# A hybrid attention and recurrence layer: two recurrent groups in step, values for four heads at once, gated outputs through DRAM, halves apart in the last output block

## The chip, the cores and the metric

The kernel runs on one core of a Trainium2 chip. The metric is the device time of one launch in microseconds, lower is better. A core has five engines with their own instruction streams: TensorE (PE in the profile; its weight loads are PEld), VectorE (DVE), ScalarE (ACT), GpSimd (POOL) and SyncE (SP), which here issues nearly all transfers. Each engine works through its stream in order and waits on semaphores for the others.

## The reference

One layer over 256 frames of width 4096, all in float32. An input projection of `x` feeds two groups of heads and a gate:

```
proj = x @ w_in                      # fox q|k|v|f, rwkv r|k|v|w_down|a_down, gate z
fox:   logits[t,s] = q_t.k_s/sqrt(128) + sum_{s<j<=t} log f_j ; softmax over s <= t ; times v      (16 heads of 128)
rwkv:  r,k,v,wd,ad are mixed with the frame before (mu_shift); decay and rate come from low-rank products
       S_t = S_{t-1} diag(w_t) + (S_{t-1} a_t) b_t^T + v_t k_t^T ;  y_t = S_t r_t                  (32 heads of 64)
       a = -kk, b = kk * rate, kk = normalised k*k_k ; GroupNorm per head of y, plus a bonus (r.k.r_k) v
h   = concat(fox, rwkv) * silu(z)
out = LayerNorm(2**0.25 * x + h @ w_out)
```

## The kernel before

**Tiling.** A group is 128 columns: one fox head and two rwkv heads; there are 16 groups. `x` lies transposed in SBUF as 32 tiles `xs[k]` of 128 x 256 frames, each split into a high and a low float32r part (2 x 256 columns). A weight tile of 128 x 1024 is fetched by SP (`fetch`, lines 206 to 211; four raw buffers `wr`), cast to its high part by ACT (line 134) and subtracted to its low part by DVE (line 135); three pairs of these are held. `mm` (lines 138 to 140) makes one k-step of a projection: the high weights times both parts of `x` (512 columns), the low weights times the high part (256 columns). `proj(i, j)` (line 221) runs 32 such k-steps for one group and one of eight projections: r, k, v of the recurrence, q, k, v of fox, and the gates of fox and rwkv.

**Side work.** All else that the mixing needs is written as Python generators (`front`, `rwkv`, `fox`). `slot()` (line 193) is called after every four k-steps and advances each generator to its next `yield`, so that its instructions are written between the projections' matmuls; `wait(n)` lets n slots pass, and the table `W` holds these numbers. The framework then orders each engine's stream by a planner that simulates durations and takes what is ready first in the order written; `keep_in_program_order` pins single instructions.

**The recurrence.** `rwkv(i)` works in four chunks of 64 frames for the two heads of one group, j = 0 and 1 on partitions 0 to 63 and 64 to 127. In order: norms `np` (lines 410, 411), Gram products `gp` (427), centred values `vp` (433), transposes `tp` (436); the masks (444, 453); the strictly lower blocks go to DRAM as `nd` and come back broadcast as `Nb`; a triangular solve by 31 row steps on DVE (473, 476); its result goes to DRAM as `td` and comes back as `T` (480, 483); `qt` (493) and `xp` (512) complete the inverses `X`. Then for each chunk: `rh` (502) is copied to `R` by DVE (504); `up` (525) is copied to `UV`, half by DVE (526) and half by ACT (527); `sp` (532) updates the state `SV` (537, 541); `yp` (544) gathers the outputs. After that the GroupNorm with `vs` (556, 557), and `gate` (330), which keeps every gated output `h` in SBUF. These small products are in plain float32 and show as two matmul records each; those of the two heads use different halves of the array.

**fox** (567) transposes its head's values (`fvp`, 577), makes the logits (`fsp`, 581 and 582), the softmax, its transposes (`fpt`, 595) and the output (`fop`, 600 and 601).

**The output.** Eight blocks of 512 columns (line 666). Each runs 32 k-steps of six matmuls of 512 columns (681 to 683), three for each half m of the frames. In the first block `get_h` (637) splits each `h` into its parts; the tail of the last group's recurrence is still between its matmuls. After the last block: the sums of both halves (696, 697), moments (709), a small row product by which mean and bias go in (721, 729), the scaling on DVE (730) and the stores (732, 735).

Of the kernel before, what the change touches and what calls it, by code (L numbers as in the profile page):

```python
# [17 lines left out]
P = 128  # L18
# [18 lines left out]
ROWS = 2  # L37
W = {"fr": 10, "fo": 3, "vs": 2, "np": 6, "gp": 5, "d1": 10, "d2": 10, "xp": 3, "fs": 4, "fp": 5}
# [39 lines left out]
def layer(ctx: ExitStack, tc: tile.TileContext, xt, xtok, w_lora, w_main, w_o, up, par, mulora, fbias, lng, lnb, cst, out, groups=G, dbg=None):  # L78
# [52 lines left out]
    def split(src, n, name):  # L131
        hi = wpool.tile([P, 1024], F32R, tag="wh", name=name + "h")
        lo = wpool.tile([P, 1024], F32R, tag="wl", name=name + "l")
# [44 lines left out]
    X = const.tile([P, NCH, P], F32, name="X")  # L178
    nc.gpsimd.memset(X, 0.0)
    gb = [const.tile([P, NCH, P], F32, name=f"gb{j}") for j in range(2)]  # L180
    for j in range(2):
        nc.gpsimd.memset(gb[j], 0.0)
# [17 lines left out]
    stream = [(f"w{i}_{j}_{q}", w_main[i, j][:, 8 * q : 8 * q + 8, :]) for i in range(groups) for j in range(8) for q in range(4) if i or j]  # L200
    if dbg is None:
        stream += [(f"wo{b}_{q}", w_o[b][:, 2 * q : 2 * q + 2, :]) for b in range(NB) for q in range(KT // 2)]
    stream.reverse()
    ready = []

    def fetch():
        if stream:
# [3 lines left out]
            ready.append((name, *split(raw, 1024, name)))  # L211
# [20 lines left out]

    mid = ctx.enter_context(ExitStack())
    hpool = mid.enter_context(tc.tile_pool(name="hpool", bufs=1))
    rp = mid.enter_context(tc.tile_pool(name="rp", bufs=1))

# [25 lines left out]

    def shifted(acc, n, i):
        name = f"s{n}_{i}"
        r = t256(f"s{n}", name)
# [53 lines left out]
    szs = {}  # L319

    def silu2(acc, key):
# [4 lines left out]
        sz = t256("sz" + key[0], key + "s")  # L326
# [3 lines left out]
    def gate(y, key, k):  # L330
        h = hpool.tile([P, S], F32, tag=f"h{k}", name=f"h{k}")
        nc.vector.scalar_tensor_tensor(h, y, 0.5, szs[key], ALU.mult, ALU.mult)
        hs[k] = h
# [12 lines left out]

    pre = {}
    done = set()

    def front(i):  # L350
# [22 lines left out]
        eL = rp.tile([P, NCH, C + 1], F32, tag="eL", name=f"eL{i}", bufs=2)  # L373
# [9 lines left out]
        pre[i] = (eL, eI, am, ae)  # L383

    def rwkv(i):
        while i not in pre or (i, 1) not in rk:
            yield
        eL, eI, am, ae = pre[i]
        r, kr = rk[i, 0], rk[i, 1]
        k = rt(f"k{i}")  # L390
# [388 lines left out]
```

## Time and profile before

| | |
|---|---|
| median of 3 runs (lowest, highest) | 2037.81 us (2037.07, 2040.23) |
| the profiled execution: its own time, its span | 2038.04 us, 2036.2 us |
| granted TensorE clock, mean | 0.996 |
| busy: PE, PEld, DVE, ACT, POOL | 2019.8, 1709.0, 1465.5, 1026.4, 27.6 us |
| data moved | 372.71 MB, mean 183 GB/s |

How to read it: the span runs from the first to the last instruction; the program's own time is 1.8 us more. PE counts as busy while a matmul is under way, and the matmuls overlap, so a row's duration (0.39 us for 512 columns) is not what a matmul costs: that is the distance between the starts of two rows. In the timeline a row is: start, duration, engine, line, operation, out<-in, shapes, how many were merged; idle time before it in brackets.

### The profile page before, as it was taken

How to read it: one execution, taken by the hardware profiler on the slowest of the kernel's cores; microseconds unless marked ns; L12 is line 12 of the kernel's file. 1: busy time of each engine (PE TensorE's matmuls, PEld its weight loads, DVE VectorE, ACT ScalarE, POOL GpSimd, SP SyncE). 2: the span in 40 equal slices, each digit the busy share in tenths (PEclk: the TensorE clock that was granted, in tenths of full speed). 3: DMA queues.
4: the chain of work that ended last, by engine and by line, in shares of the span. 5: the costliest groups of instructions: out<-in, count | busy, mean ns of one | idle time of the engine just before them, and what ended most of it. 6: DMA issues, size and time to landing. Idle time of an engine off the chain costs nothing.

```text
span 2036.2 us, 32893 instructions
## 1 busy us (share of the span) xinstructions
PE 2019.8 (99%) x12426; PEld 1709.0 (84%) x12426; DVE 1465.5 (72%) x2921; ACT 1026.4 (50%) x1609; POOL 27.6 (1%) x138
## 2 busy tenths in 40 slices
PE   9999999999999999999999999999999999999997
PEld 7888888888888888888888888888888888888885
DVE  7877777777777777777777777777777796655555
ACT  6645454545454545454545454545454564433332
POOL 0000000000000000000000000000000000000000
PEclk9999999999999999999999999999999999999998
DMA  8555555555555555555555555555555557866664
GB/s 288 181 178 177 173 178 172 179 173 177 172 177 172 179 171 179 172 179 173 178 174 177 174 177 175 175 175 173 176 172 176 172 173 243 261 194 191 186 205 145
DMA packets 131295, 372.71 MB, mean 183 GB/s; under 512 B 31208, under 2 KB 40600, under 8 KB 131136
## 3 DMA queue, kind: packets, MB, share of 16 engines
q1 hardware_dynamic: 130704, 370.19, 57.8%
q8 instruction: 97, 1.59, 0.3%
q10 hardware_dynamic: 432, 0.43, 0.1%
q14 instruction: 62, 0.51, 0.1%
HBM read 364.23 MB, written 6.32 MB: 182 GB/s over the span
## 4 chain that ended last, share of the span: by engine, by line
PE 96%; DVE 2%; DMA 1%; issue 0%; ACT 0%; SPq 0%; DVEq 0%
PE acc L139 47%; PE acc L140 23%; PE oacc L681 6%; PE oacc L682 6%; PE oacc L683 6%; PE yp L544 1%; PE gp L427 1%; PE rh L502 1%; PE sp L532 1%; PE accl L139 1%; PE up L525 1%; DMA xr<-in_xt_dram 1%; DVE res L730 0%; PE vp L433 0%; PE tp L436 0%
## 5 line engine op out<-in xcount | busy, mean ns | idle before, releaser
L139 PE MATMUL acc<-x,w_2h 128*128 128x512 f32 x1016 | 377.0, 408 | 0.0
L139 PE MATMUL acc<-x,w_1h 128*128 128x512 f32 x1016 | 369.7, 402 | 0.0
L139 PE MATMUL acc<-x,w_3h 128*128 128x512 f32 x1016 | 369.6, 401 | 0.0
L139 PE MATMUL acc<-x,w_0h 128*128 128x512 f32 x1016 | 365.5, 399 | 0.0
L140 PE MATMUL acc<-x,w_1l 128*128 128x256 f32 x1016 | 285.8, 281 | 0.0
L140 PE MATMUL acc<-x,w_3l 128*128 128x256 f32 x1016 | 284.8, 280 | 0.0
L140 PE MATMUL acc<-x,w_2l 128*128 128x256 f32 x1016 | 284.7, 280 | 0.0
L140 PE MATMUL acc<-x,w_0l 128*128 128x256 f32 x1016 | 284.6, 280 | 0.0
L139 PEld LDWEIGHTS acc<-x,w_1h 128*128 128x128 f32 x1016 | 190.7, 188 | 45.6
L139 PEld LDWEIGHTS acc<-x,w_3h 128*128 128x128 f32 x1016 | 190.7, 188 | 44.5
L139 PEld LDWEIGHTS acc<-x,w_0h 128*128 128x128 f32 x1016 | 190.7, 188 | 44.2
L139 PEld LDWEIGHTS acc<-x,w_2h 128*128 128x128 f32 x1016 | 190.9, 188 | 43.5
L134 ACT CAST w_0h<-w 128x1024 fp32r<-128x1024 f32 x127 | 133.4, 1050 | 170.1 <-PE acc L139 136.5
L135 DVE TENSOR_TENSOR w_2l<-w,w_2h 128x1024 fp32r<-128x1024 f32 x127 | 155.4, 1223 | 80.5 <-ACT w_2h L134 80.2
L134 ACT CAST w_2h<-w 128x1024 fp32r<-128x1024 f32 x127 | 133.4, 1050 | 153.4 <-PE acc L139 140.5
L140 PEld LDWEIGHTS acc<-x,w_3l 128*128 128x128 f32 x1016 | 191.9, 189 | 0.6
L140 PEld LDWEIGHTS acc<-x,w_2l 128*128 128x128 f32 x1016 | 192.1, 189 | 0.5
L135 DVE TENSOR_TENSOR w_0l<-w,w_0h 128x1024 fp32r<-128x1024 f32 x127 | 155.3, 1223 | 50.9 <-ACT w_0h L134 49.8
L140 PEld LDWEIGHTS acc<-x,w_1l 128*128 128x128 f32 x1016 | 191.9, 189 | 0.0
L140 PEld LDWEIGHTS acc<-x,w_0l 128*128 128x128 f32 x1016 | 191.8, 189 | 0.0
L135 DVE TENSOR_TENSOR w_1l<-w,w_1h 128x1024 fp32r<-128x1024 f32 x127 | 155.2, 1222 | 49.1 <-ACT w_1h L134 49.0
L134 ACT CAST w_1h<-w 128x1024 fp32r<-128x1024 f32 x127 | 132.8, 1046 | 110.8 <-issue 57.6
(703 smaller groups left out, 3240.4 us busy)
## 6 DMA issues: line engine op xcount, KB each, us to landing
w<-in_w_main_dram SPq DMA_DIRECT2D x508, 512.0 KB
wo<-in_w_o_dram SPq DMA_DIRECT2D x128, 512.0 KB
Nb<-nd SPq DMA_DIRECT2D x16, 512.0 KB
res<-in_xtok_dram SPq DMA_DIRECT2D x16, 256.0 KB
out_dram<-res SPq DMA_DIRECT2D x7, 512.0 KB
xr<-in_xt_dram SPq DMA_DIRECT2D x6, 512.0 KB
lr<-in_w_lora_dram SPq DMA_DIRECT2D x6, 416.0 KB
nb<-ncd SPq DMA_DIRECT2D x16, 128.0 KB
```

Of the source, the lines that this page charges most:

```text
L134: nc.scalar.copy(hi[:, :n], src[:, :n])
L135: nc.vector.tensor_tensor(lo[:, :n], src[:, :n], hi[:, :n].bitcast(F32), ALU.subtract)
L139: nc.tensor.matmul(acc[:m, :], hi[:, o : o + m], xs[k].rearrange("p a t -> p (a t)"), start=(k == 0), stop=False)
L140: nc.tensor.matmul(acc[:m, :S], lo[:, o : o + m], xs[k][:, 0, :], start=False, stop=(k == KT - 1))
L427: nc.tensor.matmul(gp[j][:, c * P : (c + 1) * P], BK[h, c, :], lt[j][h, c, :], start=True, stop=True)
L502: nc.tensor.matmul(rh[HALF[j], :C], lt[j][:, c, 0:C], SV[j][:, c, :], start=True, stop=True)
L525: nc.tensor.matmul(upp[:, :C], X[:, c, :], R, start=True, stop=True)
L532: nc.tensor.matmul(sp[HALF[j], :C], BKt[:, c, j * C : (j + 1) * C], UV[j][:, c, :], start=True, stop=True)
L544: nc.tensor.matmul(yp[HALF[j], c * C : (c + 1) * C], lhs[j][:, c, :], rhs[j][:, c, C:P], start=lhs is SV, stop=lhs is UV)
L681: nc.tensor.matmul(acc[m], ht[k][:, 0, tt], hi[:, o], start=(k == 0), stop=False)
L682: nc.tensor.matmul(acc[m], ht[k][:, 1, tt], hi[:, o], start=False, stop=False)
L683: nc.tensor.matmul(acc[m], ht[k][:, 0, tt], lo[:, o], start=False, stop=(k == KT - 1))
```

## The change

Six parts.

1. **Two groups in step.** `order()` gives the projections of groups i and i + 1 in turn: r, k, v of both, then the rest of both. `prepare(i)` takes the part of the recurrence up to the norms, for each group; `rwkv(n)` does the rest for both groups u = 0, 1 of pair n at once. Each burst of small matmuls holds those of both groups, and DVE and ACT handle both in one instruction where they can. The head order inside a burst is j = 1, 0. The norms and the GroupNorm take the low part first. The transposes `tp` get a burst of their own, four slots after `gp` and `vp`. GpSimd multiplies `BK` by the chunk's decay (`kept`) ahead of them, and the state's own decay is applied ahead (`sl`), so that the state update is one addition. Both halves of `UV` are copied by ACT. The solve takes one row for both groups per slot (`ROWS` 1), and the waits are set anew.
2. **Values for four heads at once.** `value(n)` has the frames' tiles as the stationary and 512 weight columns as the moving operand, so the values of four heads come out with frames on partitions; the projection j = 5 of each group and the transposes `fvp` are gone. It holds two PSUM banks while it runs.
3. **Gated outputs via DRAM.** `h` of k < 28 is stored to DRAM (`hd`) and loaded again in the first output block (`load_h`, three buffers, three ahead). The room goes to the doubled buffers.
4. **Halves apart in the last output block.** The last five weight tiles are first used for half 0 only; half 0's moments run while half 1's remaining 30 matmuls do, with the row product and four of half 0's final column blocks between them.
5. `w_v` is a new input array with the value weights; `w_main` has seven projections.
6. `X` and `gb` are doubled and move from `const` to the pool `rp`.

```diff
-ROWS = 2
-W = {"fr": 10, "fo": 3, "vs": 2, "np": 6, "gp": 5, "d1": 10, "d2": 10, "xp": 3, "fs": 4, "fp": 5}
+LATE = 5
+NPROJ = 7
+VB = OB // P
+INNER = 14
+ROWS = 1
+W = {"fo": 3, "vs": 2, "np": 6, "gp": 5, "tp": 4, "d1": 8, "d2": 12, "xp": 3, "fs": 4, "fp": 5}
...
+    def order():
+        for i in range(0, groups, 2):
+            for g in (i, i + 1):
+                for j in range(3):
+                    yield g, j
+            for g in (i, i + 1):
+                for j in range(3, NPROJ):
+                    if j == 5 and g % VB == 0:
+                        yield g, None
+                    yield g, j
...
+    def value(n):
+        acc = [pst(f"accv{n}_{m}") for m in range(2)]
+        for q in range(KT // 2):
+            hi, lo = weights(f"wv{n}_{q}")
+            for j in range(2):
+                k = 2 * q + j
+                o = slice(j * OB, (j + 1) * OB)
+                for m in range(2):
+                    tt = slice(m * P, (m + 1) * P)
+                    nc.tensor.matmul(acc[m], xs[k][:, 0, tt], hi[:, o], start=(k == 0), stop=False)
+                    nc.tensor.matmul(acc[m], xs[k][:, 1, tt], hi[:, o], start=False, stop=False)
+                    nc.tensor.matmul(acc[m], xs[k][:, 0, tt], lo[:, o], start=False, stop=(k == KT - 1))
+                slot()
+        vt = rp.tile([P, 2, OB], F32, tag="vt", name=f"vt{n}")
+        for m in range(2):
+            nc.scalar.copy(vt[:, m, :], acc[m])
+        return vt
...
+        far = k < 2 * INNER
+        h = rp.tile([P, S], F32, tag="h" if far else f"h{k}", name=f"h{k}", bufs=2 if far else 1)
...
+        if far:
+            nc.sync.dma_start(out=hd[k], in_=h)
...
+    def prepare(i):
+        n, u = divmod(i, 2)
+        while u == 0 and n and n - 1 not in done:
             yield
...
-        nc.tensor.matmul(nps, onesr, flat(sh), start=True, stop=False)
-        nc.tensor.matmul(nps, onesr, flat(sl), start=False, stop=True)
+        nc.tensor.matmul(nps, onesr, sl, start=True, stop=False)
+        nc.tensor.matmul(nps, onesr, sh, start=False, stop=True)
...
+    def rwkv(n):
+        i0 = 2 * n
+        while i0 + 1 not in prepared:
+            yield
...
+        kept = BK[:, :, 0 : NCH - 1, :]
+        nc.gpsimd.tensor_tensor(kept, kept, lc[:, :, 0 : NCH - 1].unsqueeze(3).to_broadcast([P, 2, NCH - 1, P]), ALU.mult)
...
+            for a in range(4):
+                o = B * (a % 2)
+                nc.sync.dma_start(out=nd[u, a].rearrange("c r s -> r c s"), in_=gb[a // 2][B * a : B * (a + 1), u, :, o : o + B])
+            nc.sync.dma_start(out=flat(nb[:, u]), in_=nd[u].rearrange("q c r s -> (q c) (r s)").unsqueeze(1).to_broadcast([16, NG, B * B]))
...
+        yield from wait(W["tp"])
+        BKt = rp.tile([P, 2, NCH, P], F32, tag="shl", name=f"BKt{n}")
+        for u in range(2):
+            tp = pst(f"tp{n}_{u}")
+            for c in range(NCH):
+                nc.tensor.transpose(tp[:, c * P : (c + 1) * P], BK[:, u, c, :], ident)
...
+            first = nc.vector.tensor_tensor(prod[:, :, :, s + 1 :], nb[:, :, s : s + 1, s + 1 :].to_broadcast([P, 2, NJ, w]), xc[:, :, :, s + 1 :], ALU.mult)
...
+        for u in range(2):
+            nc.sync.dma_start(out=td[u].rearrange("q c (g j) s -> (q c g) (j s)", g=NG), in_=flat(xc[:, u]))
+            for a in range(4):
+                nc.sync.dma_start(out=T[B * a : B * (a + 1), u], in_=td[u, a].rearrange("c r s -> r c s"))
...
-            rh = pst(f"rh{i}_{c}")
-            for j in range(2):
-                nc.tensor.matmul(rh[HALF[j], :C], lt[j][:, c, 0:C], SV[j][:, c, :], start=True, stop=True)
+            rh = pst(f"rh{n}_{c}")
+            for u in range(2):
+                for j in (1, 0):
+                    nc.tensor.matmul(rh[HALF[j], u * C : (u + 1) * C], lt[j][:, u, c, 0:C], SV[j][:, u, c, :], start=True, stop=True)
+            R = rp.tile([P, 2, C], F32, tag="R", name=f"R{n}_{c}", bufs=2)
+            nc.vector.tensor_copy(flat(R), rh[:, : 2 * C])
...
-            upp = pst(f"up{i}_{c}")
-            nc.tensor.matmul(upp[:, :C], X[:, c, :], R, start=True, stop=True)
-            nc.vector.tensor_copy(UV[0][HALF[0], c, :], upp[HALF[0], :C])
-            nc.scalar.copy(UV[1][HALF[1], c, :], upp[HALF[1], :C])
+            upp = pst(f"up{n}_{c}")
+            for u in range(2):
+                nc.tensor.matmul(upp[:, u * C : (u + 1) * C], X[:, u, c, :], R[:, u, :], start=True, stop=True)
+            uv = upp[:, : 2 * C].rearrange("p (u t) -> p u t", u=2)
+            for j in range(2):
+                nc.scalar.copy(UV[j][HALF[j], :, c, :], uv[HALF[j]])
             yield
...
+                sp = pst(f"sp{n}_{c}")
+                for j in (1, 0):
+                    for u in range(2):
+                        nc.tensor.matmul(sp[HALF[j], u * C : (u + 1) * C], BKt[:, u, c, j * C : (j + 1) * C], UV[j][:, u, c, :], start=True, stop=True)
...
+                        nc.vector.tensor_tensor(SV[j][h, :, c + 1, :], so, sl[h], ALU.add)
+                if 0 < c + 1 < NCH - 1:
+                    sl = rp.tile([P, 2, C], F32, tag="sl", name=f"sl{n}_{c}")
+                    for j in range(2):
+                        for u in range(2):
+                            nc.scalar.mul(sl[HALF[j], u], SV[j][HALF[j], u, c + 1, :], lc[HALF[j], u, c + 1 : c + 2])
+            for u in range(2):
+                for lhs, rhs in ((SV, lt), (UV, gb)):
+                    for j in (1, 0):
+                        nc.tensor.matmul(yp[HALF[j], u * S + c * C : u * S + (c + 1) * C], lhs[j][:, u, c, :], rhs[j][:, u, c, C:P], start=lhs is SV, stop=lhs is UV)
...
+        nc.tensor.matmul(vs, onesr, yl, start=True, stop=False)
+        nc.tensor.matmul(vs, onesr, yh, start=False, stop=True)
...
-        vp = pst(f"fvp{i}")
-        for m in range(2):
-            nc.tensor.transpose(vp[:, m * P : (m + 1) * P], v[:, m * P : (m + 1) * P], ident)
-        vt = rp.tile([P, 2, P], F32, tag="vt", name=f"vt{i}")
-        nc.scalar.copy(flat(vt), vp[:, :S])
...
+    def load_h(k):
+        if k in hin or k >= 2 * INNER:
+            return
         while k not in hs:
             slot()
+        hin[k] = rp.tile([P, S], F32, tag="hin", name=f"hin{k}", bufs=3)
+        nc.sync.dma_start(out=hin[k], in_=hd[k])
+
+    def get_h(k):
+        for n in range(k, min(k + 3, 2 * INNER)):
+            load_h(n)
+        while k not in hs:
+            slot()
+        src = hin.get(k, hs[k])
...
+                    if m and b == NB - 1 and q >= KT // 2 - LATE:
+                        late.append((k, j, hi, lo))
+                    else:
+                        project(acc[m], k, j, m, hi, lo)
...
+    def moments(m):
+        add(m, NB - 1)
...
+        nc.vector.bn_aggr(mv, st[m].rearrange("p b s -> p (b s)"))
+        nc.scalar.activation(rs, mv[:, 1:2], AF.Sqrt, bias=lneps)
+        nc.vector.reciprocal(rs, rs)
+        nc.vector.scalar_tensor_tensor(s2, mv[:, 0:1], -1.0, rs, ALU.mult, ALU.mult)
+        nc.vector.tensor_copy(zh, s2)
+        nc.vector.tensor_copy(z5[:, 0:3:2], zh.bitcast(F32).to_broadcast([P, 2]))
+        last = nc.vector.tensor_tensor(z5[:, 1:2], s2, zh.bitcast(F32), ALU.subtract)
+        rss.append(rs)
...
+    def row(m, z5):
         zp = pst(f"zp{m}")
-        nc.tensor.transpose(zp[:5, :P], z5[:, m, :], ident)
+        nc.tensor.transpose(zp[:5, :P], z5, ident)
...
+    def finish(m, b):
+        o = slice(b * OB, (b + 1) * OB)
+        wp = pp.tile([P, 512], F32, tag="pp", name=f"wp{m}_{b}") if b % 2 else pst(f"wp{m}_{b}")
+        nc.tensor.matmul(wp, l5[m], rows[:, o], start=True, stop=True)
+        nc.vector.scalar_tensor_tensor(res[m][:, o], res[m][:, o], rss[m], wp, ALU.mult, ALU.add)
...
+    z0, last = moments(0)
+    with tc.issue_after(last):
+        gain(0, NB - 1)
+    early_b = 0
+    for n, (k, j, hi, lo) in enumerate(late):
+        if n == LATE:
+            row(0, z0)
+        elif n > LATE:
+            finish(0, early_b)
+            early_b += 1
+        project(acc[1], k, j, 1, hi, lo)
+    z1, last = moments(1)
+    with tc.issue_after(last):
+        for b in range(early_b, NB):
+            finish(0, b)
+        row(1, z1)
+        gain(1, NB - 1)
+    for b in range(NB):
+        finish(1, b)
```

More of the change, by code (lines that the diff above doesn't have):

```diff
@@ L203, in layer @@
     stream.reverse()
+    kept = {f"wo{NB - 1}_{KT // 2 - LATE + n}": n for n in range(LATE - 3)}
+    rpool = None
     ready = []
@@ L210, in fetch @@
             nc.sync.dma_start(out=raw, in_=src.rearrange("p k c -> p (k c)"))
-            ready.append((name, *split(raw, 1024, name)))
+            ready.append((name, *split(raw, 1024, name, kept.get(name))))
     def weights(name):
@@ L319, in layer @@
     szs = {}
+    hd = dram.tile([2 * G, P, S], F32, name="hd")
     def silu2(acc, key):
@@ L345, in layer @@
     rk = {}
-    pre = {}
+    pairs = {}
     done = set()
+    prepared = set()
     def front(i):
@@ L568, in fox @@
+        nc.vector.reciprocal(flat(sd), flat(sd))
+        nc.vector.tensor_tensor(flat(yc), flat(yc), flat(sd), ALU.mult)
+        nc.vector.tensor_tensor(flat(yc), flat(yc), flat(bon), ALU.add)
+        for u in range(2):
+            while f"r{i0 + u}" not in szs:
+                yield
+            gate(yc[:, u], f"r{i0 + u}", 2 * (i0 + u) + 1)
+        done.add(n)
+    def fox(i, q, k, vt):
         nb = rp.tile([P, 3, P], F32, tag="nb", name=f"nb{i}")
@@ L606, in fox, with ahead @@
         gate(o, f"f{i}", 2 * i)
+    def ahead():
+        for i in range(groups):
+            yield from prepare(i)
     def chain():
         yield from forget()
-        for i in range(groups):
-            yield from rwkv(i)
-    def ahead():
-        for i in range(groups):
-            while i and i - 1 not in done:
-                yield
-            yield from wait(W["fr"] if i else 0)
-            yield from front(i)
+        for n in range(groups // 2):
+            yield from rwkv(n)
@@ L620, in layer @@
     side(ahead())
     side(chain())
-    for i in range(groups):
-        for n in range(3):
-            rk[i, n] = shifted(proj(i, n), n, i)
-        fq = t256("fq", f"fq{i}")
-        gather(proj(i, 3), fq, P, f"fqe{i}", FOX_SCALE)
-        fk = t256("fk", f"fk{i}")
-        gather(proj(i, 4), fk, P, f"fke{i}")
-        fv = t256("fv", f"fv{i}")
-        gather(proj(i, 5), fv, P, f"fve{i}")
-        side(fox(i, fq, fk, fv))
-        silu2(proj(i, 6), f"f{i}")
-        silu2(proj(i, 7), f"r{i}")
+    for i, j in order():
+        if j is None:
+            vt = value(i // VB)
+            continue
+        acc = proj(i, j)
+        if j < 2:
+            while i and i - 1 not in prepared:
+                slot()
+        if j < 3:
+            rk[i, j] = shifted(acc, j, i)
+        elif j == 3:
+            fq = t256("fq", f"fq{i}")
+            gather(acc, fq, P, f"fqe{i}", FOX_SCALE)
+        elif j == 4:
+            fk = t256("fk", f"fk{i}")
+            gather(acc, fk, P, f"fke{i}")
+        else:
+            if j == 5:
+                side(fox(i, fq, fk, vt))
+            silu2(acc, f"fr"[j - 5] + str(i))
```

342 lines of the change are left out of this document (168 added, 174 removed).

## The prediction

> **What bounds the kernel now.** I read the page first, then PE's waits, then PE's timeline over one group, last the tail.
>
> ```profile
> span 2036.2 us, 32893 instructions
> ...
> PE zp L721 <- issue: 4.3, 1, 4.3
> ...
> PE wp L729 <- DVE res L730: 1.2, 3, 0.5
> ```
>
> These two are the longest and the third longest wait of PE, and both lie behind the last output block. Before that PE always has a matmul to start, so a change is worth what it takes out of PE's stream, wherever DVE, ACT and SP stand, plus what it does to the tail. What a piece of PE's stream costs is read from starts. Below, around one chunk of the recurrence, the rows of L139 that begin a k-step of a projection:
>
> ```profile
> 557.36 0.40 PE L139 MATMUL acc<-x,w_1h 128*128 128x512 f32 x1
> 557.60 0.28 PE L140 MATMUL acc<-x,w_1l 128*128 128x256 f32 x1
> 557.80 0.34 PE L502 MATMUL rh<-SV,lt 128*64 128x64 f32 x4
> ...
> 558.52 0.40 PE L139 MATMUL acc<-x,w_1h 128*128 128x512 f32 x1
> ...
> 559.21 0.40 PE L139 MATMUL acc<-x,w_1h 128*128 128x512 f32 x1
> ...
> 559.56 0.33 PE L525 MATMUL up<-R,X 128*128 128x64 f32 x2
> ...
> 560.13 0.40 PE L139 MATMUL acc<-x,w_2h 128*128 128x512 f32 x1
> ...
> 560.83 0.40 PE L139 MATMUL acc<-x,w_2h 128*128 128x512 f32 x1
> ...
> 561.28 0.34 PE L544 MATMUL yp<-lt,SV 128*64 128x64 f32 x4
> 561.45 0.29 PE L544 MATMUL yp<-gb,UV 128*64 128x64 f32 x4
> ...
> 562.12 0.40 PE L139 MATMUL acc<-x,w_2h 128*128 128x512 f32 x1
> ```
>
> Two clean k-steps take 0.70 us (558.52 to 559.21, 560.13 to 560.83), 0.35 each. Two k-steps with a burst between take: with `rh` 1.16 (557.36 to 558.52), with `up` 0.92 (559.21 to 560.13), with `yp` 1.29 (560.83 to 562.12). So the bursts cost 0.46, 0.22 and 0.59. The rest, read in the same way:
>
> ```profile
> 540.04 0.40 PE L139 MATMUL acc<-x,w_0h 128*128 128x512 f32 x1
> 540.48 0.44 PE L512 MATMUL xp<-X,Q 32*32 32x32 f32 x16
> 540.85 0.34 PE L502 MATMUL rh<-SV,lt 128*64 128x64 f32 x4
> ...
> 541.57 0.39 PE L139 MATMUL acc<-x,w_1h 128*128 128x512 f32 x1
> ...
> 549.62 0.40 PE L139 MATMUL acc<-x,w_3h 128*128 128x512 f32 x1
> ...
> 550.06 0.36 PE L532 MATMUL sp<-UV,BKt 128*64 128x64 f32 x4
> ...
> 551.03 0.40 PE L139 MATMUL acc<-x,w_3h 128*128 128x512 f32 x1
> ...
> 583.43 0.40 PE L139 MATMUL acc<-x,w_1h 128*128 128x512 f32 x1
> ...
> 583.88 1.16 PE L427 MATMUL gp<-lt,BK 64*128 64x128 f32 x16
> ...
> 585.59 0.66 PE L436 MATMUL tp<-cs,BK 128*128 128x128 f32 x4
> ...
> 586.44 0.39 PE L139 MATMUL acc<-x,w_2h 128*128 128x512 f32 x1
> ```
>
> `sp` with `yp` (12 records): 1.41 - 0.70 = 0.71. `xp` with `rh`: 0.83. `gp`, `vp`, `tp`: 2.31.
>
> **The change part by part.**
>
> *Two groups per burst.* `yp` alone has 8 records and costs 0.59; four records of `sp` more make 0.71. So a record of this kind costs 0.03 and a burst has about 0.35 whatever it holds: the first row after L140 starts 0.20 behind it (557.60 to 557.80) where 0.12 is the step between projection rows, and the way back is as dear. Doubling a burst therefore adds only its records. Per pair of groups, two old bursts against one new: `rh` alone, 3 times, 0.92 against 0.46 + 0.12: 1.02. `up`, 4 times, two records of about 0.055 (it has no second head beside it) more: 0.11 each, 0.44. `sp`/`yp`, 3 times: 0.71 - 0.36 = 0.35 each, 1.05. `yp` alone: 0.59 - 0.24 = 0.35. `xp`/`rh`: 16 records of `xp` take 0.37 (540.48 to 540.85), so 0.83 - 0.37 - 0.12 = 0.34. `qt` has the same 16 records and, by the same fixed part, saves 0.2. `gp`/`vp`/`tp`: the records are nearly all of it (1.71 us from 583.88 to 585.59, then 0.4 of `tp`), and `tp` now makes a burst of its own: 2.31 - 2.12 - 0.1, so 0.1. `vs` nothing. Sum 3.5 per pair, times 8 pairs: 28.
>
> The TensorEngine Tiling page of the Trainium skill gives two rules that part here. Its Key Properties say that a change of tiling mode drains the engine, which is a price per burst and agrees with the 0.20 against 0.12; by it the sum stays 28. Its Instruction Overhead says that each matmul has some 60 cycles whatever its width, a price per matmul; by it nothing is saved here, since the matmuls are the same.
>
> Against the 28: the new `sp` writes both groups of one head before the other head's, so records that now run beside each other may run behind one another. Bounds: nothing, or 8 records at 0.055 in place of 0.03, 0.2 for each of 24 bursts: 4.8. I take the middle, 2.4, as no row shows this order. Left: 25.6.
>
> *Values for four heads.* It replaces 16 x 32 k-steps of 0.35, 179.2 us, by 4 x 32 x 6 = 768 matmuls of 512 columns, of the kind that the output blocks run:
>
> ```profile
> 2002.70 0.39 PE L682 MATMUL oacc<-wo_11h,h 128*128 128x512 f32 x1
> ...
> 2014.94 0.39 PE L682 MATMUL oacc<-wo_15h,h 128*128 128x512 f32 x1
> ...
> 519.73 0.38 PE L577 MATMUL fvp<-cs,fv 128*128 128x128 f32 x2
> 519.95 0.39 PE L581 MATMUL fsp<-fk,fq 128*128 128x128 f32 x2
> ```
>
> Between the first two lie 18 k-halves of three matmuls: 12.24 / 54 = 0.2267 each, 174.1 in all, 5.1 less. The transposes `fvp` go: 0.22 x 16 = 3.5. It moves the same weight bytes at the same pace, and its two PSUM banks are taken while the chain is in its row steps, which use no PSUM: counted in slots, `value` begins where the 31 rows begin and ends one slot after them.
>
> *Norms, low part first.* Before, L410 is sent as soon as the high part is there, and L411 in a gap of its own:
>
> ```profile
> 576.90 0.40 PE L139 MATMUL acc<-x,w_3h 128*128 128x512 f32 x1
> 577.33 0.50 PE L411 MATMUL np<-sbl,onesr 128*128 128x512 f32 x1
> ...
> 577.78 0.40 PE L139 MATMUL acc<-x,w_3h 128*128 128x512 f32 x1
> ```
>
> This k-step takes 0.88, so L411 costs 0.53, where 512 columns cost 0.23; 0.43 instead of 0.23 pass between the first two starts, so 0.2 of it is waiting for `sbl`. Together and without that wait it saves 0.3; if PE still comes too early, 0.1. Taken 0.2 x 16 = 3.
>
> *Tail.*
>
> ```profile
> 2014.91 1.36 DVE L696 SCALAR_TENSOR_TENSOR res<-res,oacc 128x512 f32<-128x512 f32 x2 [5.39 <-PE oacc L683]
> ...
> 2015.17 0.39 PE L683 MATMUL oacc<-wo_15l,h 128*128 128x512 f32 x1
> ...
> 2021.27 10.62 DVE L730 SCALAR_TENSOR_TENSOR res<-res,rs,wp 128x512 f32<-128x512 f32 x16 [1.54 <-PE wp L729]
> ```
>
> From the last matmul to the last scaling it is 16.7 us: 6.1 (2015.17 to 2021.27) for moments and row of both halves, 10.6 for 16 blocks of 0.66. After: half 0's moments lie under 30 matmuls (6.8 us); its row product and four blocks enter PE's stream, some 2 us with four changes of shape and back; then half 1's moments, about 3.5 (6.1 less the other half's addition of 0.68, its statistics and the scaling by the gain, which cost about the same each); four blocks of half 0 and a gain, 3.3; eight blocks, 5.3. Sum 14.1: 2.6 less, between 0 and 5.
>
> *What is added.* POOL's product on `BK`, SP's queue, and the loads of `h`. The nearest rows are, in this order, POOL's elementwise work, the two ends of a round trip through DRAM, and the stretch with the most traffic:
>
> ```profile
> L573 POOL TENSOR_SCALAR_AFFINE_SELECT nb<-nb 128x128 f32<-128x128 f32 x32 | 14.1, 441 | 879.8 <-DMA nb<-ncd 713.6 <-PE acc L140 56.1 <-DVE Q L497 55.4
> ...
> 526.73 0.33 SPq L480 DMA_DIRECT2D td<-xc  x1
> ...
> 529.52 1.76 SPq L483 DMA_DIRECT2D T<-td  x4
> ...
> 1700.00:1740.00 40.00, 40.00 (x179) 33.10 (x178) 26.09 (x29) 17.87 (x19) 0.00 (x0) 1.00 0.86 283
> ```
>
> 441 ns for 128 elements: 2.6 us for the 768 of this product. `tp` waits for it and all of PE's stream stands behind `tp`, but four slots of four k-steps (5.6 us) lie between, so it is counted at nothing. At three times the price, 7.8, the loss would be 8 x 2.2 = 18.
>
> SP's queue: `td` and `T` are sent for one group and then for the other. From `td` to the last `T` it is 4.55 us now, 9.1 for two, and weight loads stand behind. Four raw buffers hold 4 x 2.8 = 11.2 us of PE's work (eight k-steps each), so it is hidden, narrowly. The stores of `h` are 28 issues over 1600 us.
>
> The first output block: each k-step now needs 256 KB of weights and 128 KB of `h` in six matmuls, 1.36 us: 289 GB/s. 283 were moved at 0.86 busy, so the engines nearly suffice. The three load buffers turn over in about 2.8 us (from `td` to `T`, a store that has landed) plus the split by ACT and DVE, twice 0.35 (half of the 0.68 that 512 columns took DVE at 2014.91): 3.5, or 1.2 us per k-step; and the first loads can run before the block. If a load took twice that 2.8, it would be 2.1 per k-step, and 28 x 0.75 = 21 late, less the 11 us of the last projection in which loads can run ahead, and less the bursts: some 8. Bounds 0 and 8, taken 1. For the longer steps of the chain (both `UV` copies behind one another on ACT, behind a cast of weights), 2: the planner lets other matmuls pass while it thinks that they are not ready, and the 0.2 at `sbl` is what it was wrong by.
>
> **Sum.** 25.6 + 5.1 + 3.5 + 3 + 2.6 - 3 = 36.8. The profiled execution took 2038.04 (1.8 more than its span); the median of the runs is 0.2 below. 2037.8 - 36.8 = 2001.
>
> **The rivals.**
>
> *The chain's waits come back.* Each dependent step now handles two groups, while a slot is as long as before. If PE waits 0.2 (as for `sbl`) at each of some 13 bursts of a pair, 8 x 13 x 0.2 = 21 of the gain go: 2022. For it: that row. Against it: the other bursts start at the same distance behind their last projection row as those whose data were long there, so they do not wait now, and one copy fewer changes engines.
>
> *The price sits in each matmul.* Pairing then saves nothing, and 5.1 + 3.5 + 3 + 2.6 - 3 = 11 are left: 2027. Against it: 8 against 12 records. It is the second rule of the page named above.
>
> *Cheaper bursts yet.* With head 1 first, the first matmul of a burst waits for what came last and the others for nothing. If that takes 0.08 more off the 13 bursts of a pair and `sp` loses nothing: 8.3 + 2.4 more, 1990. The 0.20 before `yp` alone, whose inputs are old, speaks for the change of shape and not the wait.
>
> *SP starves PE* (slower). The two round trips stand behind one another, twice per pair (`nd` and `td`), and weights behind them. Up to 11.2 us nothing happens. From there PE stands still, in 16 places; when a trip is 13.5 us rather than 9.1, the loss is 37 and the gain is gone. At 15 us: 16 x 3.8 = 61, so 2062. Against it: in between the planner can send weights, as it does now between `td` and `T`.
>
> **How the numbers follow.** Forecast 0.60. Waits 0.17, of which 0.02 end within 0.2% of before. Per matmul 0.05. Cheaper 0.12. Slower 0.06, a tenth of it mild. What a measurement tells from no change is 0.2%, 4 us. Faster 0.92, same 0.02, slower 0.06. The forecast's own bounds (`sp` 2.4, `np` 1.5, tail 2.5, first block 7) make 1992 to 2014; the range takes in the cheaper case and that of the waits: 1985 to 2023, and leaves out the slower one and the last.
>
> **What would show it.** `rh` x8 in a distance of about 1.28 between the L139 rows around it, and not 1.6; `up` x4 1.03; `sp`/`yp` x24 1.77, or 1.97 if `sp` runs one behind the other. `np`'s two rows 0.23 apart. `value` as 43.5 us of rows 0.2267 apart. The first output block no longer than the 43.5 us of its matmuls and its bursts. Wrong would be PE waits on `UV`, `T`, `BK` or weight casts in the middle of the span, or more than 14 us behind the last accumulating matmul.

## The result, and the profile after

The changed kernel takes 1994.14 us (median of 4 runs, 1992.68 to 1996.72), the kernel before, on the same chip, 2039.02 (2037.07 to 2040.79): ratio 0.978, 95% interval 0.977 to 0.979, so 44.9 us faster. The forecast was 2001, in a range of 1985 to 2023. The profiled execution took 1994.67 us, 1.8 more than its span, as before.

The span and PE's longest waits after the change (waits: engine, line, what it waited for, us in all, times, longest):

```profile
span 1992.9 us, 31562 instructions
```

```profile
PE acc L145 <- DVE w_2l L140: 4.0, 3, 1.8
PE zp L851 <- DVE z L845: 2.1, 1, 2.1
...
PE oacc L778 <- ACT h L752: 0.5, 2, 0.3
...
PE oacc L779 <- DVE h L753: 0.3, 1, 0.3
```

The first row and the two on `h` are new; `zp` belongs to the tail. Where the 43.3 us of the span (2036.2 to 1992.9) went, stage by stage, from the starts of the output's matmuls: the projections end at 1614.95 where they ended at 1660.10 (45.2 earlier); the first output block is 4.0 longer (54.64 against 50.65), mostly as the last *pair's* bursts lie in it and no longer the last group's, and in part by the waits on `h`; blocks 1 to 6 take 43.52 each as before; the last block is 2.7 longer and what follows it 4.8 shorter.

PE's timeline around one chunk of a pair (start, us, engine, line, what):

```profile
593.37 0.39 PE L144 MATMUL acc<-x,w_3h 128*128 128x512 f32 x1
...
593.76 0.66 PE L613 MATMUL up<-R,X 128*128 128x64 f32 x4
...
594.66 0.40 PE L144 MATMUL acc<-x,w_0h 128*128 128x512 f32 x1
595.04 0.46 PE L622 MATMUL sp<-UV,BKt 128*64 128x64 f32 x8
...
595.67 0.29 PE L638 MATMUL yp<-gb,UV 128*64 128x64 f32 x4
...
596.46 0.40 PE L144 MATMUL acc<-x,w_0h 128*128 128x512 f32 x1
...
596.81 0.40 PE L144 MATMUL acc<-x,w_0h 128*128 128x512 f32 x1
597.05 0.28 PE L145 MATMUL acc<-x,w_0l 128*128 128x256 f32 x1
597.26 0.45 PE L586 MATMUL rh<-SV,lt 128*64 128x64 f32 x8
597.65 0.50 PE L144 MATMUL acc<-x,w_0h 128*128 128x512 f32 x1
597.99 0.28 PE L145 MATMUL acc<-x,w_0l 128*128 128x256 f32 x1
598.10 0.40 PE L144 MATMUL acc<-x,w_0h 128*128 128x512 f32 x1
```

Two k-steps with `rh` x8 between take 1.29 us (596.81 to 598.10; forecast 1.28), with `sp` and `yp` x24 1.80 (594.66 to 596.46; forecast 1.77, or 1.97 if `sp` lost its overlap), with `up` x4 1.29 (593.37 to 594.66, the dearest of its kind; the mean is 1.20, forecast 1.03). Taken over all of them, less two clean k-steps of 0.347 each (the mean is 0.351 before and 0.350 after, by which each row would be about 0.01 less), in us:

| burst | before, per group | after, per pair | saved per pair |
|---|---|---|---|
| `rh`, 3 times | 0.468 | 0.583 | 1.06 (forecast 1.02) |
| `sp`/`yp`, 3 times | 0.737 | 1.079 | 1.19 (1.05) |
| `yp` alone | 0.595 | 0.820 | 0.37 (0.35) |
| `up`, 4 times | 0.230 | 0.51; 0.39 to 0.45 where `fpt` or `fop` joins it | none (0.44) |
| `xp`/`rh` | 0.837 | 1.209 | 0.46 (0.34) |
| `qt` | 0.573 | 0.831 | 0.32 (0.20) |
| `gp`, `vp`, `tp` | 2.317 | 3.272 + 0.890 | 0.47 (0.10) |
| `vs` | 0.269 | 0.473 | 0.07 (0) |

The 0.737 is a mean of 0.71, where `sp`/`yp` stands alone, and 0.80 in the 15 bursts that follow `up` at once. In all it is 3.9 per pair, 31.3 for the kernel; forecast were 28, less 2.4 for `sp`. In PE's own order the matmuls outside the projections and output blocks stood in 337 bursts before and stand in 199 now.

A norm, and the values of four heads (their first row, and the k-step that follows their last):

```profile
525.32 0.39 PE L260 MATMUL accv<-wv_0h,x 128*128 128x512 f32 x1
...
568.66 0.39 PE L262 MATMUL accv<-wv_15l,x 128*128 128x512 f32 x1
568.88 0.39 PE L144 MATMUL acc<-x,w_0h 128*128 128x512 f32 x1
...
682.21 0.39 PE L144 MATMUL acc<-x,w_3h 128*128 128x512 f32 x1
...
682.55 0.40 PE L474 MATMUL np<-shl,onesr 128*128 128x512 f32 x1
682.79 0.39 PE L475 MATMUL np<-shl,onesr 128*128 128x512 f32 x1
683.02 0.39 PE L144 MATMUL acc<-x,w_3h 128*128 128x512 f32 x1
```

The values take 43.56 (525.32 to 568.88), 0.2269 for each of 192 matmuls, as forecast. The norm costs 0.46 (0.81 less a k-step) and its rows stand 0.24 apart; over the 15 groups whose norm stands alone it costs 0.505, against 0.777 before in two pieces. Whether that is the order of its two parts is a question for the runs below.

The tail, from all engines' timeline:

```profile
1976.68 0.40 PE L780 MATMUL oacc<-wo_15l,h 128*128 128x512 f32 x1
...
1977.12 0.69 DVE L788 SCALAR_TENSOR_TENSOR res<-res,oacc 128x512 f32<-128x512 f32 x1
...
1980.09 2.71 DVE L860 SCALAR_TENSOR_TENSOR res<-res,rs,wp 128x512 f32<-128x512 f32 x4
...
1983.33 5.35 DVE L860 SCALAR_TENSOR_TENSOR res<-res,rs,wp 128x512 f32<-128x512 f32 x8
```

From the last matmul to the last scaling it is 12.0 (1976.68 to 1988.68), where 16.7 had been; the row product and four blocks in PE's stream cost 2.7. Together 14.7, where 14.1 were forecast, 2 of them in the stream.

### The profile page after: what moved, and what is told of

It reads as the page before. It is cut to its first block, busy times and chain, and to the rows that moved or that the text cites. A ratio compares the mean times of both kernels' runs of the same rounds, so it can differ in the third digit from the quotient of the medians.

```text
span 1992.9 us, 31562 instructions
## 1 busy us (share of the span) xinstructions
PE 1975.3 (99%) x12122; PEld 1680.0 (84%) x12122; DVE 1369.0 (69%) x2181; ACT 987.7 (50%) x1514; POOL 45.8 (2%) x132
## 5 line engine op out<-in xcount | busy, mean ns | idle before, releaser
L144 PE MATMUL acc<-x,w_2h 128*128 128x512 f32 x888 | 323.3, 402 | 0.0
L144 PE MATMUL acc<-x,w_3h 128*128 128x512 f32 x888 | 320.2, 399 | 0.0
L144 PE MATMUL acc<-x,w_0h 128*128 128x512 f32 x888 | 319.7, 398 | 0.0
L144 PE MATMUL acc<-x,w_1h 128*128 128x512 f32 x888 | 319.4, 399 | 0.0
L145 PE MATMUL acc<-x,w_2l 128*128 128x256 f32 x888 | 248.7, 280 | 4.0 <-DVE w_2l L140 4.0
L145 PE MATMUL acc<-x,w_0l 128*128 128x256 f32 x888 | 248.9, 280 | 0.0
L145 PE MATMUL acc<-x,w_1l 128*128 128x256 f32 x888 | 248.4, 280 | 0.0
L145 PE MATMUL acc<-x,w_3l 128*128 128x256 f32 x888 | 248.2, 280 | 0.0
L145 PEld LDWEIGHTS acc<-x,w_2l 128*128 128x128 f32 x888 | 167.5, 189 | 5.9 <-DVE w_2l L140 5.2
L140 DVE TENSOR_TENSOR w_3l<-w,w_3h 128x1024 fp32r<-128x1024 f32 x111 | 135.7, 1222 | 47.4 <-ACT w_3h L139 46.1
```

Source lines behind the costliest of these rows:

```text
L144: nc.tensor.matmul(acc[:m, :], hi[:, o : o + m], xs[k].rearrange("p a t -> p (a t)"), start=(k == 0), stop=False)
L145: nc.tensor.matmul(acc[:m, :S], lo[:, o : o + m], xs[k][:, 0, :], start=False, stop=(k == KT - 1))
```

## The experiments

All ratios are to the kernel before, run beside it on the same chip; the changed kernel's is 0.978. The experiments ran on three chips, on which the kernel before took 2038.3 to 2039.4 us, so a difference between the medians of two edited kernels holds to about 1 us. Four edits that turned out to be worth nothing lie at 1992.9 to 1995.1, which shows what the medians tell apart.

### The bursts apart again

```diff
             for u in range(2):
+                if u:
+                    yield
                 for j in (1, 0):
...
+            if sp is None:
+                values(0)
+                yield
+                values(1)
+            else:
+                states(0)
+                values(0)
+                yield
+                states(1)
...
+                values(1)
```

The first part is in `rh`; `states(u)` sends the `sp` of one group and `values(u)` its `yp`.

> The changed kernel, but rh, sp and yp of the two groups of a pair are sent one slot apart, so the same matmuls make 64 bursts more (32 of rh, 24 of sp with yp, 8 of yp alone; the last pair's in the first output block among them); up stays joined. Burst theory (a burst has a fixed price of about 0.35 us, a record 0.03): rh 32 x 0.35, sp/yp 24 x 0.40, yp 8 x 0.37 make 23.8 us more than the changed kernel, about 2018. Price-per-matmul theory: no difference, 1994. If the joined bursts had only hidden waits of the chain: less than 10 us more, with new waits of PE on DVE or ACT.

Measured 2015.08 us, ratio 0.988 (0.987 to 0.990): 20.9 more than the changed kernel. PE's timeline of this kernel:

```profile
598.28 0.40 PE L144 MATMUL acc<-x,w_3h 128*128 128x512 f32 x1
...
598.72 0.34 PE L588 MATMUL rh<-SV,lt 128*64 128x64 f32 x4
...
599.44 0.40 PE L144 MATMUL acc<-x,w_3h 128*128 128x512 f32 x1
```

1.16 for two k-steps with `rh` x4 (598.28 to 599.44), just what it was in the kernel before, and each pair has two of them. Over all: `rh` 0.468, `sp`/`yp` 0.702, `yp` 0.583. Two such bursts less one joined burst give the fixed price: 0.353, 0.325 and 0.346 us. 32, 24 and 8 of them make 21.9; 20.9 were measured. In this run's trace the waits on `w_2l` are gone and PE waits 4.3 us for the norms' low parts (`shl`) instead; the two nearly cancel in the 20.9, and the price itself is read from the bursts. The price per burst is shown. The TensorEngine Tiling page of the Trainium skill (Key Properties) says that a change of tiling mode drains the engine; this agrees, and about 0.35 us is what entering and leaving cost here.

### More matmuls in a burst

```diff
-                for j in (1, 0):
+                for j in (1, 0, 1, 0):
```

> The changed kernel with rh's eight matmuls of each of its 32 bursts sent twice, the same products into the same place; no burst more. Burst theory (0.029 us a record): 8 x 32 x 0.029 = 7.4 us slower, 2001.5. Price-per-matmul theory (0.583 for eight records, 0.073 each, or 0.117 each by the four records of the kernel before): 18.7 to 30 us slower, 2013 to 2024.

Measured 2000.83, ratio 0.982 (0.980 to 0.983): 6.7 more. In PE's timeline of this kernel:

```profile
601.17 0.40 PE L144 MATMUL acc<-x,w_0h 128*128 128x512 f32 x1
...
601.61 0.69 PE L586 MATMUL rh<-SV,lt 128*64 128x64 f32 x16
...
602.68 0.39 PE L144 MATMUL acc<-x,w_0h 128*128 128x512 f32 x1
```

`rh` costs 0.817 (1.51 less two k-steps) where eight records cost 0.583: 0.029 a record. The four runs of this kernel lie between 1997.96 and 2004.13, so it is the rows and not the 6.7 that carry this. The rival of a price in each matmul falls with these two runs.

### Head order, and the order of `sp`

```diff
-                for j in (1, 0):
+                for j in (0, 1):
```

(in `rh`, `sp` and `yp`)

> The changed kernel with head 0 ahead of head 1 again in rh, sp and yp, as the kernel before had it; nothing else. Theory: the bursts start with a fixed price for the change of shape and wait for nothing, so the order of heads is worth nothing: within 1.5 us of 1994. Rival (the first matmul of a burst meets the latest operand, 0.08 us at each of some 13 bursts of a pair): 8.3 us slower, 2002.

Measured 1995.08, ratio 0.979 (0.977 to 0.980). The order of the heads is worth nothing that shows here.

```diff
-                for j in (1, 0):
-                    for u in range(2):
+                for u in range(2):
+                    for j in (1, 0):
```

> The changed kernel with sp sent group by group, so that the two heads take turns, and not both groups of one head before the other's. The forecast held that the changed order costs 2.4 us (0.1 for each of 24 bursts): 1991.7. Theory by the changed kernel's trace (the burst of 24 records takes 1.079, as forecast without that loss): no difference, within 1 us of 1994.

Measured 1992.91, ratio 0.978 (0.976 to 0.979); its bursts of 24 cost 1.072 against 1.079. The 2.4 us that the forecast took off for `sp` never were there.

### The norms

```diff
-        nc.tensor.matmul(nps, onesr, sl, start=True, stop=False)
-        nc.tensor.matmul(nps, onesr, sh, start=False, stop=True)
+        nc.tensor.matmul(nps, onesr, sh, start=True, stop=False)
+        nc.tensor.matmul(nps, onesr, sl, start=False, stop=True)
```

(and so for `vs`)

> The changed kernel with the high part's matmul ahead of the low part's again, in np and in vs. Theory: each np falls into two bursts again, the second at 0.245 us where it had to wait for the low part; 16 x 0.27 = 4.4 us slower, 1998.5, all of it in np. Rival (np's gain came from something else in the change): within 1 us of 1994.

Measured 1993.98, ratio 0.978 (0.977 to 0.980). The expectation fell: with the old order 12 of 16 norms still stand in one burst, at 0.467, and four in two pieces. In these four the order does save something, about 0.14 each (0.80 in two pieces against 0.66), some 0.6 us in all; the gain of 0.3 in each of the others is not from the order. The other side of it, an edit of the kernel before:

```diff
-        nc.tensor.matmul(nps, onesr, flat(sh), start=True, stop=False)
-        nc.tensor.matmul(nps, onesr, flat(sl), start=False, stop=True)
+        nc.tensor.matmul(nps, onesr, flat(sl), start=True, stop=False)
+        nc.tensor.matmul(nps, onesr, flat(sh), start=False, stop=True)
```

> The kernel before with one edit: the low part's matmul ahead of the high part's in np. In the kernel before the low part is there 1.46 us after the high part and np is sent as soon as it can be. Theory (the order brings the two together where the casts are late, and only there): one burst in place of two, 16 x 0.27 = 4.3 us faster than before, 2034, less what is still waited for the low part. Rival (np came together in the changed kernel only because the groups are prepared ahead; the order is worth nothing): no difference, 2038.

Measured 2040.72 against 2039.35, ratio 1.0008 (0.9999 to 1.0017). PE's timeline in this kernel:

```profile
576.42 0.40 PE L139 MATMUL acc<-x,w_3h 128*128 128x512 f32 x1
...
577.17 0.47 PE L410 MATMUL np<-sbl,onesr 128*128 128x512 f32 x1 [0.24 <-DVE sbl L398]
577.48 0.39 PE L411 MATMUL np<-sbh,onesr 128*128 128x512 f32 x1
577.71 0.39 PE L139 MATMUL acc<-x,w_3h 128*128 128x512 f32 x1
```

The parts stand together, and the wait stands in front of them: 0.24 each, and the joined burst with its wait costs 0.935 where the two pieces cost 0.777. What the changed kernel does differently is seen at the casts. DVE's timeline before, and after:

```profile
576.59 0.68 DVE L398 TENSOR_TENSOR sbl<-sb,sbh 128x512 fp32r<-128x512 f32 x1
```

```profile
679.83 0.69 DVE L462 TENSOR_TENSOR shl<-sb,shl 128x512 fp32r<-128x512 f32 x1
```

Before, the low part ends at 577.27 and its matmul starts at 577.33: PE was there first. After, it ends at 680.52, 2.0 ahead of its matmul at 682.55; about so it is in 12 of the 16 groups. In the first group of pairs 0, 2, 4 and 6 only 0.05 lie between, and these four are the ones that fall apart in the run with the high part first. `prepare(i)` runs ahead of the pair's chain, so that most casts are old when PE comes. A positive test, in the kernel before:

```diff
-W = {"fr": 10, "fo": 3, "vs": 2, "np": 6, "gp": 5, "d1": 10, "d2": 10, "xp": 3, "fs": 4, "fp": 5}
+W = {"fr": 10, "fo": 3, "vs": 2, "np": 10, "gp": 5, "d1": 6, "d2": 10, "xp": 3, "fs": 4, "fp": 5}
```

> The kernel before with np four slots (16 k-steps) later behind its casts and the next pause of the chain four slots shorter; the high part's matmul still first. Theory: np cost 0.777 in two bursts because the high part was sent 0.4 us after its cast, 1.4 us before the low part was there; later, both parts lie ready, and the two make one burst of 0.47 as in the changed kernel: 16 x 0.3 = 4.9 us faster than before, 2034. Rival (the lateness has nothing to do with it): no difference, 2039.

Measured 2045.60 against 2038.31, ratio 1.0036 (1.0023 to 1.0049): slower. At `np` the theory holds, in this kernel's timeline:

```profile
582.67 0.39 PE L139 MATMUL acc<-x,w_1h 128*128 128x512 f32 x1
...
583.01 0.40 PE L410 MATMUL np<-sbh,onesr 128*128 128x512 f32 x1
583.25 0.39 PE L411 MATMUL np<-sbl,onesr 128*128 128x512 f32 x1
583.48 0.39 PE L139 MATMUL acc<-x,w_1h 128*128 128x512 f32 x1
```

One burst of 0.464 in 15 of 16 groups, with the high part first. But the whole time went the other way, by new waits:

```profile
PE acc L140 <- DVE w_3l L135: 4.2, 10, 0.8
PE qt L493 <- DMA T<-td: 1.7, 2, 1.0
```

What follows `np` on DVE now meets the casts of weights, and the shorter pause no longer covers the way of `T` through DRAM. By their idle time these waits make 5.9 us of the some 12 between the 4.9 gained at `np` and the 7.3 lost in all. By starts they cost more: the late k-steps of the projections 9.2 over clean ones, `qt` 2.2 more than before. The first output block is 1.9 longer. So "lateness splits the norm" is shown at the burst, and a gain in the whole time by that edit is not.

### The values

```diff
-NPROJ = 7
+NPROJ = 8
...
+        vp = pst(f"fvp{i}")
+        for m in range(2):
+            nc.tensor.transpose(vp[:, m * P : (m + 1) * P], v[:, m * P : (m + 1) * P], ident)
...
-            vt = value(i // VB)
...
+            fv = t256("fv", f"fv{i}")
+            gather(acc, fv, P, f"fve{i}")
```

> The changed kernel with the values projected head by head again (eight projections per group, gathered, transposed by fvp), the rest as changed. Theory: fvp's 16 pairs of transposes (16 x 0.22 = 3.5) and 512 k-steps of 0.347 to 0.351 in place of 768 matmuls of 0.2269 (177.7 to 179.7 against 174.2: 3.5 to 5.5) come back: 7.0 to 9.0 us slower, 2001 to 2003. Rival (the value form costs as much as it saves, since its two banks hold back the chain): within 2 us of 1994.

Measured 2009.78, ratio 0.986 (0.984 to 0.987): 15.6 more, where 7 to 9 were expected. PE's waits show what came on top:

```profile
PE oacc L779 <- ACT h L753: 2.9, 5, 0.7
...
PE oacc L780 <- DVE h L754: 1.7, 4, 0.4
```

These 4.6 us lie in the first output block: the splits of `h` wait for its loads from DRAM, which turn over in three buffers. The chain had come to its end earlier here: none of the last pair's bursts, which stretch this block in the changed kernel, stands in it, and with them the cover of the loads is gone. Five buffers for them in place of three:

```diff
-        hin[k] = rp.tile([P, S], F32, tag="hin", name=f"hin{k}", bufs=3)
+        hin[k] = rp.tile([P, S], F32, tag="hin", name=f"hin{k}", bufs=5)
...
-        for n in range(k, min(k + 3, 2 * INNER)):
+        for n in range(k, min(k + 5, 2 * INNER)):
```

> The kernel with values head by head, which was 15.6 us slower than the changed one and not 7 to 9, with five load buffers for h in the first output block in place of three. Theory: 4.6 of the surplus are PE's waits on the splits of h, which turn over in three buffers at some 1.75 us per k-step; the values' form by itself is worth the 9 forecast. With five buffers the nine waits go: 4.6 us faster than that kernel, 2005. Rival (the loads themselves or ACT and DVE are the limit in the first block): within 1 us of 2010.

Measured 2003.02, ratio 0.983 (0.981 to 0.984): 6.8 less, and no wait of PE on `h` is left. The first block went from 51.31 to 43.70 us. Neither kernel has a small burst in this block, so these 7.6 are the waits alone: 4.6 is their idle time, and around each of them the starts fall some 0.3 further behind. (The rest of the trace is 2.2 longer, so that the profiled executions differ by 5.4.)

What remains to the changed kernel is 8.9, which is what the values' form was expected to be worth. It is a net of more, though: this kernel has none of the changed kernel's waits on `w_2l` and `h`, and its clean k-steps take 0.3519 in mean where the changed kernel's take 0.3499, 7.1 us over 3552 of them, for a reason that stays open. So the gain of the values rests on the rows (43.56 for four heads against 128 k-steps of 0.351, and `fvp`), and that 8.9 agrees with them is in part luck.

### The tail

```diff
-                    if m and b == NB - 1 and q >= KT // 2 - LATE:
-                        late.append((k, j, hi, lo))
-                    else:
-                        project(acc[m], k, j, m, hi, lo)
+                    project(acc[m], k, j, m, hi, lo)
...
+    add(0, NB - 1)
+    add(1, NB - 1)
```

> The changed kernel with the two halves of the last output block side by side and their moments together, as before the change. Theory: the last block is 2.7 us shorter and what follows the last accumulating matmul 4.8 us longer (16.2 to 21.0): 2.1 us slower, 1996. Rival (the tail is worth the whole of what is left after the bursts and values, some 5 us): 1999.

Measured 1995.89, ratio 0.979 (0.978 to 0.980): 1.8 more, which by itself is no more than the edits worth nothing lie apart. The trace settles it: the last matmul stands 21.1 us before the end against 16.2, and the last block is 2.7 shorter.

### The new wait on weights

In the changed kernel, ACT's timeline, then DVE's, then PE's, around the first of the three waits:

```profile
465.90 0.41 ACT L406 CAST uph<-upt 96x256 fp32r<-96x256 f32 x1 [1.80 <-DMA upt<-in_up_dram]
466.22 0.47 ACT L417 ACTIVATE tw<-lp,half 128x256 f32<-128x256 f32 x1
```

```profile
466.71 0.29 DVE L421 TENSOR_SCALAR tw<-tw 128x256 f32<-128x256 f32 x1 [1.19 <-ACT tw L417]
...
468.93 1.20 DVE L140 TENSOR_TENSOR w_2l<-w,w_2h 128x1024 fp32r<-128x1024 f32 x1
```

```profile
470.18 0.39 PE L145 MATMUL acc<-x,w_2l 128*128 128x256 f32 x1 [1.01 <-DVE w_2l L140]
```

ACT stands 1.8 us for a small load, `tw` comes late, DVE stands 1.19 for it, and the low part of the weights queues behind: PE stands 1.01. By starts the three k-steps with these waits take 1.63, 2.45 and 1.81 us where a clean one takes 0.35: 4.8 in all, for 4.0 of idle time. The PSUM page of the Trainium skill (Engine vs sequencer instructions) says that the queues of ScalarE and VectorE are strictly first in, first out; these rows agree.

```diff
     def front(i):
-        upt = rp.tile([LORA, 2, P], F32, tag="upt", name=f"upt{i}")
-        nc.sync.dma_start(out=upt, in_=up[i])
...
+        load_up(i + 1)
```

(`load_up` allots the buffer and sends the load; it now stands behind the use of `upt`.)

> The changed kernel with the 96 x 256 up-projection weights of the next group fetched as soon as their buffer is free (first row of the group's front in the kernel as changed, about 24 slots earlier here). Theory: the three waits of PE on w_2l of 1.0, 1.8 and 1.2 us come from the cast of these weights standing on ACT for its DMA, so they go: 4 us faster, 1990. Rival (ACT and DVE are simply full at these places): the waits stay with another releaser, within 1 us of 1994.

Measured 1994.86, ratio 0.978 (0.977 to 0.980): no difference. The edit missed its aim. `front` of a pair's two groups run one right behind the other, the one buffer came free only then, and the cast still stood for the load. So:

```diff
-INNER = 14
+INNER = 15
...
+            upts[i] = rp.tile([LORA, 2, P], F32, tag="upt", name=f"upt{i}", bufs=2)
...
     def front(i):
-        upt = rp.tile([LORA, 2, P], F32, tag="upt", name=f"upt{i}")
-        nc.sync.dma_start(out=upt, in_=up[i])
+        load_up(i + 1)
```

> The changed kernel with two buffers for the up-projection weights, fetched a whole group ahead (room for it from one more group's outputs via DRAM). The run with one buffer fetched them no earlier: the load still came 3.9 us before its cast, since the buffer came free only then. Theory: the cast on ACT no longer stands 1.5 to 1.8 us for this DMA, so the three waits of PE on w_2l (4.0 us in the profile of the changed kernel, 2.1 and 1.8 in two others) go: 2 to 4 us faster, 1990 to 1992. Rival (DVE is full at these places, with a reciprocal of 1.75 and the casts of weights): the waits stay within 0.5 us of what they were, 1994.

Measured 1991.85 (1989.47 to 1992.74), ratio 0.977 (0.975 to 0.978), PE's longest waits:

```profile
PE zp L860 <- DVE z L854: 2.1, 1, 2.1
...
PE acc L145 <- DVE w_0l L140: 0.8, 1, 0.8
```

All three waits on `w_2l` are gone, and the projections end 2.1 us earlier. The 0.8 on `w_0l` lies in the first k-step of the projections and is there only in the two kernels that fetch these weights ahead. What one more group's outputs through DRAM (`INNER` 15) cost is not separated. It is the fastest median of all, 2.3 below the changed kernel's; the two intervals overlap a little, so the waits' cause is shown and the gain of 2 us is likely, not more. The idle time of the three waits also differs from run to run: 4.0 in the profile of the changed kernel, and 2.8, 2.1, 1.8, 2.4, 4.3 and 4.1 in the six other profiles that have all three, whose edits do not touch their cause or, with one buffer, leave it. The mean is 3.1.

## Why the prediction was right, and where not

The sum came out by its main terms: PE's stream sets the time, and what leaves it is gained. Term by term, forecast against the trace: bursts 25.6 against 31.3; values 5.1 against 5.4 (512 k-steps of 0.351, the mean over the projections of the kernel before, less 174.2); `fvp` 3.5 against 3.5; norms 3 against 4.4; tail 2.6 against 2.1; new waits -3 against -4.8 by their idle time, or -6.6 by starts (4.8 for `w_2l`, 1.8 in the first output block). One gain was not in the sum: a single burst of `fpt` that cost 0.8 more than the others in the kernel before, where PE stood for the logits:

```profile
PE fpt L595 <- DVE lg L591: 0.6, 1, 0.6
```

With the waits by idle time the terms make 42.7 of the 43.3, and by starts 40.9. The clean k-steps, 0.3509 in mean before and 0.3499 after, add some 3.4 over the 3552 that are left. So the account closes to about 1 us; that 42.7 comes nearer is luck.

**Two groups per burst.** Right in its mechanism, as the runs with split bursts and with doubled `rh` show, and mis-sized in four terms. Its 0.35 for a burst was right too, but not the reading beside it, 0.20 in place of 0.12 on the way in and the way back "as dear", which makes 0.16: in the rows of `rh` x8 above, 0.09 is lost on the way in, and on the way back, besides the pause before it, the first row of the projection holds the next one up by another 0.1 (597.65 to 597.99, where 0.24 is usual). The 2.4 for `sp` was a cost that isn't there. `gp`/`vp`/`tp` was taken for records alone, at 0.1; it saves 0.47. `xp`/`rh` and `qt` were each 0.12 too low. Against that, `up` saves nothing, where 0.44 per pair was forecast: the step that took 0.055 for each of its records was wrong. Four cost about twice what two cost. In PE's timeline of the changed kernel:

```profile
599.17 0.55 PE L613 MATMUL up<-R,X 128*128 128x64 f32 x4
599.55 0.50 PE L687 MATMUL fpt<-cs,lg 128*128 128x128 f32 x3
```

0.38 pass for four, close to 0.1 each. `up` fills the whole array, as the projections do, and no price of its own for a burst is seen: four of its records cost 0.453 where they stand alone in the run with split bursts, twice the 0.230 of two. The eight records of `tp`, of the same shape, cost 0.890 in a burst of their own, 0.11 each. The TensorE: Matmul & The Clock Gate page of the Trainium skill (LDWEIGHTS) gives a weight load as its columns divided by 1.2, in ns: by it an estimate is 107 ns for the 128 columns of `up` and 53 for the 64 of `rh`, or 27 a record if two tiles load beside each other. The distances of 0.1 and 0.029 lie near these. The trace's own rows of weight loads last longer, 186 to 192 ns for `up` and 132 to 138 ns for `rh`, and overlap; that the weight load is what spaces the records is argued, not shown.

**Norms, low part first.** The size was nearly right and the step was wrong. It read the 0.2 that passed before L411 as a price of the order. Where the casts are late, in the kernel before, the order alone gives nothing: the wait moves in front of the pair. The gain is from the part of the change that the forecast cost at nothing there, the preparing of groups ahead of the chain. A wait is removed by making its operand early, not by asking for it first or last.

**Values, `fvp`.** Right: 8.9 by the rows (5.4 and 3.5) against 8.6.

**Tail.** Right: 14.7 against 14.1, and 2.1 gained in the span against 2.6; the run without this part gives 1.8, and by its trace the same two shifts. The share in PE's stream was 0.7 too low.

**New waits.** The forecast put 2 on the chain's longer steps, at `UV`; in the profile of the changed kernel PE never waits for `UV`. What came is 4.0 of idle time, 4.8 by starts, in a place that was not named: `front`'s load of 96 x 256 weights, its cast on ACT, and the subtraction on DVE behind it. For the first output block 1 was taken, with bounds of 0 and 8; 0.8 (0.5 and 0.3) of idle time was measured, 1.8 by starts. That their sum came anywhere near the 3 is luck, as the larger wait stands in another place for another cause. The cover named for the loads, the bursts, fits: in the changed kernel the waits begin at 1657, after the last burst at 1639, and where the chain ended earlier, in the kernel with values per head, the same three buffers cost 7.6 by starts (4.6 of idle time).

**Hidden work.** POOL's product takes 1.73 us, where 2.6 were estimated:

```profile
L501 POOL TENSOR_TENSOR BK<-BK,lc 128x768 f32<-128x768 f32 x8 | 13.9, 1734 | 39.0 <-PE gp L498 39.0
```

Nothing waits for it. SP does not starve PE: nearly always the casts of weights wait for PE to give their buffers back, and not for a load:

```profile
L139 ACT CAST w_2h<-w 128x1024 fp32r<-128x1024 f32 x111 | 116.7, 1051 | 148.2 <-PE acc L144 138.0
```

In the projections two casts stood for a load of such weights, 4.1 us together, and PE waited for neither.

**The rivals.** The chain's waits did not come back as a whole; one wait of the kind did, in three places. The price per matmul is refuted. The cheaper bursts by head order are refuted, though the time came near what that rival gave (1990) for other reasons. SP's rival did not occur.

## What to carry to other kernels

Where small matmuls of another tile shape stand between large ones, count the bursts, not the matmuls: what is joined saves the fixed price, and what has the large ones' shape (`up`) saves nothing. Before crediting the order of two instructions with a gain, see when their operands were there; if PE came first, the order moves the wait more than it removes it. Work hidden under something that moves (the loads of `h` under the chain's end) is priced once with that cover and once without. And a wait costs more than the idle time that the list of waits gives it: by starts it was 4.8 for 4.0, 7.6 for 4.6.

## What was not expected of the hardware

A burst of 128 x 64 tiles has a fixed price of 0.33 to 0.35 us, and inside it a record costs 0.029. A record of 64 columns over the whole array costs about 0.1, more than three times as much. And one small load, for which ACT stood 1.8 us, stopped PE for 1.0, two engines further on.
